# Ordering the scaling of the residual rows behind the convolution in the up projection

## The chip, the core and the metric

The kernel runs on one core of a Trainium2 chip. The time is what the device takes for one execution, in microseconds (us), as the median of several runs. The engines of the core that matter here: TensorE (PE, matmuls; its weight loads are listed apart as PEld), VectorE (DVE), ScalarE (ACT), GpSimd (POOL) and SyncE (SP), which issues most DMA loads. Each engine works through its own queue of instructions in order and waits on semaphores for the others.

## What is computed

One decoder layer on 512 positions of width 1024: two attention branches, an output projection, a LayerNorm, and a gated MLP with a causal convolution of width 3 between the up projection and the gate. All of it is float32. The part that the change touches:

```python
x = _layer_norm(DEEPNORM_ALPHA * x + (1.0 + gt1) * attn_out, ln1_g, ln1_b)
u2 = x * (1.0 + sc2) + sh2
h = _causal_depthwise_conv(u2 @ w_up, conv_w, conv_b)
h_gate, h_val = jnp.split(h, 2, axis=-1)
ffn_out = (jax.nn.silu(h_gate) * h_val) @ w_down
x = _layer_norm(DEEPNORM_ALPHA * x + (1.0 + gt2) * ffn_out, ln2_g, ln2_b)
```

The second LayerNorm needs x itself, scaled by the first one's gain and shifted by its bias (both times alpha). The up projection needs it only in the form u2, which is made apart.

## The kernel before

**Stages.** The kernel runs the modulation and the input projection, attention, the output projection, the up projection (here some 375 to 660 us of the span), and the last products of the down projection with the second LayerNorm.

**Precision.** Each float32 operand is split into a high part (ACT, a cast, for instance wh, line 217) and a low part (DVE, a subtraction at line 94, for instance wl). A product is three matmuls, high by high, low by high and high by low (lines 152 to 154), so every third matmul of a tile in the up projection reads wl.

**Tiles of the up projection.** The loop over n = 0 to 43 (`for n in range(2 * FT)`) makes 44 tiles of 128 channels by 512 positions, each with 24 matmuls of 128x512 into one PSUM bank taken by `bank()`. There are eight banks. From n = 7 on, six of them are held by the accumulators of `early_products`, which adds 18 matmuls after every fourth tile (n = 7, 11, 15, ...; lines 1148 to 1150). The tiles take the remaining two in turn.

**Convolution.** Each tile is followed by its convolution: one ACT instruction (line 1201) and two DVE instructions (lines 1202 and 1203) that read the bank. The list `convs` holds the second DVE instruction of each tile. After every second tile comes the gate (lines 1209 and 1210); after every fourth, the blocks of the down product (lines 1129 to 1132) and their splits (fo, hv).

**Scaling of the residual rows.** `x1` holds four blocks of 128 positions, in two halves of 512 channels each. `o_x1(i, e)` multiplies one half by the gain row (line 975) and adds the bias row (line 976), both on DVE. With its first call it loads the two rows in halves, broadcast over 128 partitions (`ln_row`: four loads on SyncE, line 913, and four scalings on ACT, lines 916 and 919). The loop calls it at every second tile from n = 6 to 20. What uses the result are the sums of the last phases (`fold`, line 1234).

**Other work of DVE in this stage.** The sums of weight blocks for the down product (`pair_proc`, lines 997 to 1002, with splits wdl), the weighted sums of the modulation (`mod_sum`, line 240), and a row of gates (lines 646 and 649).

**Order.** SyncE's queue follows the program. The other engines' instructions are put in order by a scheduler when the program is built: it takes what it expects to be ready, and what is written first needn't stand first. `tc.issue_after(x)` makes what is recorded inside it stand behind x.

Of the kernel before, what the change touches and what calls it, by code (L numbers as in the profile page):

```python
# [12 lines left out]
ALU = mybir.AluOpType  # L13
# [38 lines left out]
def layer_kernel(ctx: ExitStack, tc: tile.TileContext, out, xT, x, c8, wa0, wa1, bcol, w1, wct, wv, bf,  # L52
# [3 lines left out]
    V, S, G, PE = nc.vector, nc.scalar, nc.gpsimd, nc.tensor  # L56
# [20 lines left out]
    def bank():  # L77
        return pp.tile([P, 512], F32, name=nm("ps"), tag="ps")
# [78 lines left out]
    reads, held, pins, convs = [], [], {}, []  # L157
# [752 lines left out]
    def ln_row(n):  # L910
        t = [z(F32, "lnr") for _ in range(2)]
        for e in range(2):
            nc.sync.dma_start(t[e], lnrow[n : n + 1, e * 512 : (e + 1) * 512].broadcast_to([P, 512]))
        if n % 2 == 0:
            for e in range(2):
                S.activation(t[e], t[e], AF.Copy, scale=-0.5 * ALPHA)
        else:
            for e in range(2):
                S.activation(t[e], t[e], AF.Copy, scale=ALPHA)
        return t  # L920
# [3 lines left out]
    x1 = []  # L924
    lnr = []
# [46 lines left out]
    def o_x1(i, e):  # L972
        if not lnr:
            lnr.extend([ln_row(0), ln_row(1)])
        V.tensor_tensor(x1[i][e], x1[i][e], lnr[0][e], ALU.mult)
        V.tensor_tensor(x1[i][e], x1[i][e], lnr[1][e], ALU.add)

    def raw_proc(r):
        return r
# [191 lines left out]
    for n in range(2 * FT):  # L1171
        if n < NSPLIT:
            h, l = items[wui[n]][4]
            ps = bks[n]
            up_mm(ps, h, l, slice(256, 512))
        else:
            ps = bank()
            h, l = weights(wui[n], min(LOADS - 1, wui[min(n + 2, 2 * FT - 1)] - wui[n]))
            up_mm(ps, h, l, slice(0, 512))
            if n % 2 == 0 and 6 <= n < 22:  # L1180
                o_x1((n - 6) // 4, n // 2 % 2 == 0)
            if n >= 7 and n % 4 == 3:
                early_products((n - 7) // 4)
            if n in (10, 28):
                weights(wai[n], 0)
            if n in (10, 30):
                rows = gate_rows(1 + n // 30, G)
                next(rows)
            if n in (11, 32):
                next(rows)  # L1190
        if n == 24:
            for i in range(2):
                lnr2.append(lnp.tile([P, D], F32, name=f"ln2_{i}", tag=f"ln2_{i}"))
                nc.sync.dma_start(lnr2[i], lnrow[2 + i : 3 + i, :].broadcast_to([P, D]))
        if n == 28:
            S.activation(lnr2[0], lnr2[0], AF.Copy, scale=-0.5)
        if n in (30, 32):
            S.dma_start(out[(n - 30) * 64 : (n - 30) * 64 + P, :], lnr2[1])
        t = z(F32, "cv")
        hc.append(t)  # L1200
        S.activation(t, ps, AF.Identity, bias=cw[:, n, 3:4], scale=cw[:, n, 2:3])  # L1201
        V.scalar_tensor_tensor(t[:, 1:], ps[:, 0:511], cw[:, n, 1:2], t[:, 1:], ALU.mult, ALU.add)  # L1202
        convs.append(V.scalar_tensor_tensor(t[:, 2:], ps[:, 0:510], cw[:, n, 0:1], t[:, 2:], ALU.mult, ALU.add))  # L1203
        if n > 3:
            next(work, None)
        if n % 2 == 1:
            g, v = hc
            hc = []
            S.activation(g, g, AF.Silu)  # L1209
            V.tensor_tensor(g, g, v, ALU.mult)  # L1210
            hs.append(g)
            if n % 4 == 3:
                work = blocks(*hs)
                hs = []
                if n < 2 * FT - 1:
                    next(work)
# [102 lines left out]
    lnr = lnr2  # L1319
# [110 lines left out]
```

## Time and profile before

| | |
|---|---|
| median of 3 runs | 735.07 us (734.85 to 735.47) |
| profiled execution | 734.44 us |
| its span | 732.6 us |
| PE busy | 723.3 us, 99% of the span |
| DVE busy | 600.7 us, 82% |
| ACT busy | 391.6 us, 53% |
| granted clock of PE, mean | 0.998 |

The profile is of one execution, and its times count from the start of its span. An engine's busy time counts each stretch in which at least one instruction runs. Matmuls are pipelined, so that the row of a matmul (0.39 us) overlaps the next; how fast PE is going shows in the starts. On DVE too the next instruction may start some 0.08 us before the row of the last one ends, so that the distance between two starts is a little less than a duration. What matters of a wait is whose wait it is: an idle DVE costs nothing as long as PE goes on.

### The profile page before, as it was taken

Reading aid. Unit: us, or ns where it says so; the run is one execution under the profiler, and the core shown is the slowest. Engines: PE = TensorE matmul, PEld = TensorE weight load, DVE = VectorE, ACT = ScalarE, POOL = GpSimd, SP = SyncE. Lnnn points to the kernel's source line nnn. Section 1 sums busy time; section 2 is a strip of 40 time slices with the busy share of each in tenths; the row PEclk is TensorE's granted clock in tenths of the full one; section 3 lists DMA queues with packets and bytes.
Section 4 is the critical chain, followed back from the end, with each engine's and each line's share of the span. In section 5 each row is a group of like instructions: output and inputs, shape, how many; then the busy total and the mean of one; then the engine's idle time right before and its main releaser. Section 6 shows DMA issues by size and latency. Waiting matters only on the chain.

```text
span 732.6 us, 9845 instructions
## 1 busy us (share of the span) xinstructions
PE 723.3 (99%) x3444; PEld 602.2 (82%) x3444; DVE 600.7 (82%) x1041; ACT 391.6 (53%) x684; POOL 87.9 (12%) x142
## 2 busy tenths in 40 slices
PE   8999999999999999999999999999999999999996
PEld 5878888888888888888889888888888888888885
DVE  7978799778898886873687999977887787679996
ACT  5576466686885754442056553454453444347550
POOL 1045224352010000000000001000011010000010
PEclk9999999999999999999999999999999999999999
DMA  9953535423332241632075677577799777656734
GB/s 357 404 207 126 174 116 198 148 88 115 118 116 103 71 171 59 221 130 86 1 259 146 209 248 245 166 247 229 206 339 254 211 239 208 200 161 226 223 86 95
DMA packets 45490, 131.96 MB, mean 180 GB/s; under 512 B 6168, under 2 KB 7200, under 8 KB 45440
## 3 DMA queue, kind: packets, MB, share of 16 engines
q1 hardware_dynamic: 38176, 112.61, 44.7%
q0 software_dynamic: 4224, 10.30, 7.0%
q10 hardware_dynamic: 3040, 8.42, 3.1%
q8 instruction: 27, 0.44, 0.2%
q14 instruction: 23, 0.19, 0.1%
HBM read 118.39 MB, written 12.85 MB: 179 GB/s over the span
## 4 chain that ended last, share of the span: by engine, by line
PE 97%; DMA 1%; DVE 1%; ACT 0%; issue 0%; DVEq 0%
PE ps L152 19%; PE ps L154 19%; PE ps L153 19%; PE ps L1148 5%; PE ps L1149 5%; PE ps L1150 5%; PE ps L369 5%; PE ps L613 3%; PE ps L595 2%; PE ps L521 2%; PE ps L523 2%; PE ps L522 2%; PE ps L939 2%; PE ps L940 2%; PE ps L941 2%; PE ps L547 1%
## 5 line engine op out<-in xcount | busy, mean ns | idle before, releaser
L217 ACT ACTIVATE wh<-raw 128x1024 fp32r<-128x1024 f32 (+1 forms) x105 | 109.1, 1041 | 106.2 <-PE ps L153 44.3
L94 DVE TENSOR_TENSOR wl<-raw,wh 128x1024 fp32r<-128x1024 f32 (+2 forms) x114 | 137.2, 1204 | 33.2 <-ACT wh L217 32.4
L152 PE MATMUL ps<-u2h,wh 128*128 128x512 f32 (+1 forms) x376 | 141.4, 376 | 0.0
L153 PE MATMUL ps<-u2l,wh 128*128 128x512 f32 (+1 forms) x376 | 141.2, 375 | 0.0
L154 PE MATMUL ps<-u2h,wl 128*128 128x512 f32 (+1 forms) x376 | 141.2, 375 | 0.0
L154 PEld LDWEIGHTS ps<-u2h,wl 128*128 128x128 f32 x376 | 70.8, 188 | 12.8
L152 PEld LDWEIGHTS ps<-u2h,wh 128*128 128x128 f32 x376 | 70.8, 188 | 12.8
L153 PEld LDWEIGHTS ps<-u2l,wh 128*128 128x128 f32 x376 | 70.8, 188 | 12.6
L152 PE MATMUL ps<-uh,wh 128*128 128x512 f32 x200 | 79.5, 398 | 0.0
L154 PE MATMUL ps<-uh,wl 128*128 128x512 f32 x200 | 78.3, 391 | 0.0
L153 PE MATMUL ps<-ul,wh 128*128 128x512 f32 x200 | 77.9, 390 | 0.0
L1201 ACT ACTIVATE cv<-ps,cw 128x512 f32<-128x512 f32 x44 | 34.0, 773 | 46.6 <-PE ps L154 40.2
L1202 DVE SCALAR_TENSOR_TENSOR cv<-ps,cw,cv 128x511 f32<-128x511 f32 x44 | 32.8, 744 | 22.6 <-ACT cv L1201 22.6
L154 PEld LDWEIGHTS ps<-uh,wl 128*128 128x128 f32 x200 | 37.5, 188 | 8.6 <-DVE wl L94 0.3
L153 PEld LDWEIGHTS ps<-ul,wh 128*128 128x128 f32 x200 | 37.6, 188 | 7.4
L152 PEld LDWEIGHTS ps<-uh,wh 128*128 128x128 f32 x200 | 37.5, 188 | 7.4
L240 DVE SCALAR_TENSOR_TENSOR raw<-raw,cbc 128x1024 f32<-128x1024 f32 x32 | 39.5, 1238 | 0.0
L575 POOL TENSOR_TENSOR pt<-pt,om 128x127 f32<-128x127 f32 (+3 forms) x32 | 38.6, 1218 | 1.4 <-DVE om L574 1.3
L181 POOL DMA_DIRECT2D raw<-in_wdp x10 | 8.8, 885 | 245.1 <-DMA raw<-in_wdp 229.2
L1203 DVE SCALAR_TENSOR_TENSOR cv<-ps,cw,cv 128x510 f32<-128x510 f32 x44 | 32.7, 743 | 0.4
L574 DVE TENSOR_TENSOR_SCAN om<-om,dg 128x127 f32<-128x127 f32 (+3 forms) x32 | 28.8, 960 | 3.8 <-ACT om L569 3.8
L1209 ACT ACTIVATE cv<-cv 128x512 f32<-128x512 f32 x22 | 13.9, 631 | 33.0 <-DVE cv L1203 33.0
(245 smaller groups left out, 1550.1 us busy)
## 6 DMA issues: line engine op xcount, KB each, us to landing
raw<-in_wup SPq DMA_DIRECT2D x44, 512.0 KB, 5.1
raw<-in_wa SPq DMA_DIRECT2D x32, 512.0 KB, 3.5
raw<-in_wct SPq DMA_DIRECT2D x25, 512.0 KB, 4.5
raw<-in_wdp SPq DMA_DIRECT2D x20, 512.0 KB, 5.2
wa<-in_wa SPq DMA_DIRECT2D x16, 512.0 KB, 8.7
raw<-in_wdp SPq DMA_DIRECT2D x22, 256.0 KB, 4.6
raw<-t SPq DMA_DIRECT2D x22, 256.0 KB, 4.1
raw<-in_wdp POOLq DMA_DIRECT2D x10, 512.0 KB, 7.3
```

What stands on the lines that cost most here:

```text
L94: state["read"] = V.tensor_tensor(o, i, fl(hi), ALU.subtract)
L152: PE.matmul(ps, wh, ah, start=first, stop=False)
L153: PE.matmul(ps, wh, al, start=False, stop=False)
L154: return PE.matmul(ps, wl, ah, start=False, stop=last)
L217: state["hi"] = S.activation(h[:, 0:cols], r[:, 0:cols], AF.Copy)
L240: state["read"] = V.scalar_tensor_tensor(wt[:, c], wt[:, c], 1.0, cbc[:, c] if by is None else by, ALU.mult, ALU.mult, accum_out=o)
L369: m = PE.matmul(grp[g], w, u, start=j == 0 and n == 0, stop=j == KT - 1 and n == 2)
L575: G.tensor_tensor(pt[b][:, s : e - 1], pt[b][:, s : e - 1], om[:, s + 1 : e], ALU.mult)
L1148: PE.matmul(ps, ah, bh, start=first, stop=False, skip_group_check=onto)
L1149: PE.matmul(ps, ah, bl, start=False, stop=False, skip_group_check=onto)
L1150: return PE.matmul(ps, al, bh, start=False, stop=last, skip_group_check=onto)
L1201: S.activation(t, ps, AF.Identity, bias=cw[:, n, 3:4], scale=cw[:, n, 2:3])
```

## The change

The scaling pairs of `o_x1` are recorded inside `tc.issue_after(convs[-1].ins)`. `convs[-1]` is the second DVE instruction of the convolution of the tile before, since the call stands ahead of the tile's own convolution in the loop. The calls move by two tiles: n = 8 to 22 in place of 6 to 20, every second tile as before, with the same halves in the same order. All instructions are the same ones, 16 scalings, four loads and four ACT scalings. Lines from 976 on count one more.

```diff
--- before.py
+++ after.py
@@ -972,8 +972,9 @@
     def o_x1(i, e):
         if not lnr:
             lnr.extend([ln_row(0), ln_row(1)])
-        V.tensor_tensor(x1[i][e], x1[i][e], lnr[0][e], ALU.mult)
-        V.tensor_tensor(x1[i][e], x1[i][e], lnr[1][e], ALU.add)
+        with tc.issue_after(convs[-1].ins):
+            V.tensor_tensor(x1[i][e], x1[i][e], lnr[0][e], ALU.mult)
+            V.tensor_tensor(x1[i][e], x1[i][e], lnr[1][e], ALU.add)
 
     def raw_proc(r):
         return r
@@ -1177,8 +1178,8 @@
             ps = bank()
             h, l = weights(wui[n], min(LOADS - 1, wui[min(n + 2, 2 * FT - 1)] - wui[n]))
             up_mm(ps, h, l, slice(0, 512))
-            if n % 2 == 0 and 6 <= n < 22:
-                o_x1((n - 6) // 4, n // 2 % 2 == 0)
+            if n % 2 == 0 and 8 <= n < 24:
+                o_x1((n - 8) // 4, n // 2 % 2 == 1)
             if n >= 7 and n % 4 == 3:
                 early_products((n - 7) // 4)
             if n in (10, 28):
```

What the scheduler makes of it, at three places in DVE's queue. A convolution's instruction names its tile by the buffer cv_; xn_ are the residual rows, lnr_ the gain and bias rows. Numbers of buffers differ between the two programs.

First listing: from the convolution of tile 8 (cv_4296 before, cv_4294 now) to that of tile 9 (cv_4350, cv_4348). Before:

```order
L1203 SCALAR_TENSOR_TENSOR cv_4296<-ps_4260,cw,cv_4296 128x510
L94 TENSOR_TENSOR fo_4301<-cv_4187,fh_4300 128x256
L999 TENSOR_TENSOR raw_4309<-raw_4309 128x512
L94 TENSOR_TENSOR wdl_4319<-raw_4309,wdh_4317 128x512
L94 TENSOR_TENSOR wl_4379<-raw_4372,wh_4378 128x1024
L94 TENSOR_TENSOR wdl_4320<-raw_4309,wdh_4318 128x512
L975 TENSOR_TENSOR xn_3452<-xn_3452,lnr_4173 128x512
L646 SCALAR_TENSOR_TENSOR gcol<-modr,bcols 128x4
L1202 SCALAR_TENSOR_TENSOR cv_4350<-ps_4306,cw,cv_4350 128x511
L94 TENSOR_TENSOR hv_4354<-cv_4058,hv_4354 128x256
L1203 SCALAR_TENSOR_TENSOR cv_4350<-ps_4306,cw,cv_4350 128x510
```

Now:

```order
L1204 SCALAR_TENSOR_TENSOR cv_4294<-ps_4246,cw,cv_4294 128x510
L94 TENSOR_TENSOR fo_4299<-cv_4173,fh_4298 128x256
L999 TENSOR_TENSOR raw_4307<-raw_4307,raw_4247 128x512
L94 TENSOR_TENSOR wl_4377<-raw_4370,wh_4376 128x1024
L1000 TENSOR_TENSOR raw_4307<-raw_4307 128x512
L94 TENSOR_TENSOR wdl_4317<-raw_4307,wdh_4315 128x512
L240 SCALAR_TENSOR_TENSOR raw_4374,modr<-raw_4374,cbc 128x1024
L94 TENSOR_TENSOR wdl_4318<-raw_4307,wdh_4316 128x512
L94 TENSOR_TENSOR wl_4381<-raw_4372,wh_4380 128x1024
L1203 SCALAR_TENSOR_TENSOR cv_4348<-ps_4304,cw,cv_4348 128x511
L94 TENSOR_TENSOR hv_4352<-cv_4058,hv_4352 128x256
L1204 SCALAR_TENSOR_TENSOR cv_4348<-ps_4304,cw,cv_4348 128x510
```

Between the two convolutions the scaling L975 and the small L646 are gone, and the first sum (L999, before L998, which stood ahead of tile 8's convolution), the weighted sum L240 and one more wl split have come in.

Second listing: from tile 24's convolution on, with the wl split of tile 26 (wl_5214). Before:

```order
L1203 SCALAR_TENSOR_TENSOR cv_5198<-ps_5160,cw,cv_5198 128x510
L94 TENSOR_TENSOR fo_5203<-cv_5093,fh_5202 128x256
L94 TENSOR_TENSOR wl_5214<-raw_5209,wh_5213 128x1024
L997 TENSOR_TENSOR wg_5217<-raw_5211,gt_4412 128x512
L998 TENSOR_TENSOR raw_5211<-raw_5211,raw_5161 128x512
L999 TENSOR_TENSOR raw_5211<-raw_5211 128x512
```

Now:

```order
L1204 SCALAR_TENSOR_TENSOR cv_5198<-ps_5160,cw,cv_5198 128x510
L94 TENSOR_TENSOR fo_5203<-cv_5093,fh_5202 128x256
L998 TENSOR_TENSOR wg_5217<-raw_5211,gt_4410 128x512
L999 TENSOR_TENSOR raw_5211<-raw_5211,raw_5161 128x512
L94 TENSOR_TENSOR wl_5214<-raw_5209,wh_5213 128x1024
L1000 TENSOR_TENSOR raw_5211<-raw_5211 128x512
```

The product wg and the first sum stand ahead of the wl split now, and stood behind it.

Third listing: the blocks after tile 19, and tile 20's convolution (cv_4973, cv_4971). Before:

```order
L1130 TENSOR_TENSOR sg_926_4931<-cv_4869,cv_4747 128x256
L1131 TENSOR_TENSOR cv_4747<-sg_926_4931,cv_4747 128x256
L1132 TENSOR_TENSOR sg_927_4932<-cv_4747,cv_4869 128x256
L94 TENSOR_TENSOR wl_4989<-raw_4984,wh_4988 128x1024
L94 TENSOR_TENSOR wdl_4944<-raw_4941,wdh_4943 128x512
L94 TENSOR_TENSOR wl_5060<-raw_5053,wh_5059 128x1024
L1202 SCALAR_TENSOR_TENSOR cv_4973<-ps_4937,cw,cv_4973 128x511
L94 TENSOR_TENSOR fo_4978<-cv_4747,fh_4977 128x256
L1203 SCALAR_TENSOR_TENSOR cv_4973<-ps_4937,cw,cv_4973 128x510
```

Now:

```order
L976 TENSOR_TENSOR xn_3668<-xn_3668,lnr_4280 128x512
L1131 TENSOR_TENSOR sg_926_4929<-cv_4867,cv_4745 128x256
L977 TENSOR_TENSOR xn_3668<-xn_3668,lnr_4286 128x512
L1132 TENSOR_TENSOR cv_4745<-sg_926_4929,cv_4745 128x256
L94 TENSOR_TENSOR wl_4987<-raw_4982,wh_4986 128x1024
L1133 TENSOR_TENSOR sg_927_4930<-cv_4745,cv_4867 128x256
L94 TENSOR_TENSOR wl_5058<-raw_5051,wh_5057 128x1024
L94 TENSOR_TENSOR wdl_4942<-raw_4939,wdh_4941 128x512
L1203 SCALAR_TENSOR_TENSOR cv_4971<-ps_4935,cw,cv_4971 128x511
L94 TENSOR_TENSOR fo_4976<-cv_4745,fh_4975 128x256
L1204 SCALAR_TENSOR_TENSOR cv_4971<-ps_4935,cw,cv_4971 128x510
```

A pair of scalings (L976, L977) has come in among the blocks, and the wdl split stands behind the second wl split.

On SyncE's queue the four loads of the gain and bias rows stood ahead of four weight loads (for a weighted sum, for tile 9, and for two blocks of the down weights) and stand behind them now. On GpSimd's queue the four writes and the read of the gate row stand ahead of one accumulating load that they stood behind. On PE some of the early products' matmuls change place with matmuls of the tile next to them. No scaling is left in a crowd ahead of tile 12's convolution, where before the last ten of the sixteen stood among nineteen instructions.

## Rows read from the trace of the kernel before

**Rows 1.** Head of the page: span, then busy time and share of each engine.

```profile
span 732.6 us, 9845 instructions
...
PE 723.3 (99%) x3444; PEld 602.2 (82%) x3444; DVE 600.7 (82%) x1041; ACT 391.6 (53%) x684; POOL 87.9 (12%) x142
```

**Rows 2.** Waits of PE, whole span: waiter <- releaser, total us, times, longest.

```profile
PE ps L229 <- DVE warm L107: 1.2, 1, 1.2
PE ps L229 <- DVE wa L240: 0.3, 1, 0.3
PE ps L369 <- DVE uh L331: 0.3, 1, 0.3
```

**Rows 3.** Table by stretch: length, busy us (instructions) by engine, PEclk, DMA share, GB/s.

```profile
421.60:460.40 38.80, 38.80 (x172) 32.12 (x172) 36.95 (x65) 17.72 (x28) 4.39 (x7) 1.00 0.74 237
...
538.00:576.80 38.80, 38.80 (x173) 32.15 (x172) 33.15 (x56) 20.10 (x34) 5.17 (x7) 1.00 0.93 282
```

**Rows 4.** Instructions on the LayerNorm rows: ns min/median/max, first to last start.

```profile
L975 DVE TENSOR_TENSOR xn<-xn,lnr x8: 677/682/683, 421.6 to 459.0; 128x512 f32<-128x512 f32 x8
...
L913 SPq DMA_DIRECT2D lnr<-in_lnrow x4: 376/400/432, 410.6 to 412.1; - x4
```

**Rows 5.** Timeline of PE at tile 12: start us, us, instruction, [idle before <-releaser].

```profile
453.61 0.39 PE L152 MATMUL ps<-u2h,wh 128*128 128x512 f32 x1
453.84 0.39 PE L153 MATMUL ps<-u2l,wh 128*128 128x512 f32 x1
```

**Rows 6.** Timeline of DVE, end of tile 12's convolution.

```profile
462.45 0.74 DVE L1203 SCALAR_TENSOR_TENSOR cv<-ps,cw,cv 128x510 f32<-128x510 f32 x1
```

**Rows 7.** First sum into the scaled rows: ns min/median/max, first to last start.

```profile
L1234 DVE TENSOR_TENSOR xn<-xn,tm x2: 681/682/682, 675.0 to 678.3; 128x512 f32<-128x512 f32 x2
```

**Rows 8.** Timeline of DVE ahead of and in tile 20's convolution.

```profile
511.80 1.23 DVE L94 TENSOR_TENSOR wl<-raw,wh 128x1024 fp32r<-128x1024 f32 x1 [1.49 <-ACT wh L217]
...
513.93 0.74 DVE L1203 SCALAR_TENSOR_TENSOR cv<-ps,cw,cv 128x510 f32<-128x510 f32 x1
```

**Rows 9.** Timeline of DVE from tile 8's convolution to past tile 9's.

```profile
433.95 0.69 DVE L998 TENSOR_TENSOR raw<-raw,raw 128x512 f32<-128x512 f32 x1 [0.68 <-DMA raw<-in_wdp]
434.56 0.74 DVE L1202 SCALAR_TENSOR_TENSOR cv<-ps,cw,cv 128x511 f32<-128x511 f32 x1
...
437.75 1.22 DVE L94 TENSOR_TENSOR wl<-raw,wh 128x1024 fp32r<-128x1024 f32 x1
438.88 0.69 DVE L94 TENSOR_TENSOR wdl<-raw,wdh 128x512 fp32r<-128x512 f32 x1
439.49 0.68 DVE L975 TENSOR_TENSOR xn<-xn,lnr 128x512 f32<-128x512 f32 x1
...
440.16 0.74 DVE L1202 SCALAR_TENSOR_TENSOR cv<-ps,cw,cv 128x511 f32<-128x511 f32 x1
...
441.16 0.74 DVE L1203 SCALAR_TENSOR_TENSOR cv<-ps,cw,cv 128x510 f32<-128x510 f32 x1
...
445.62 1.18 DVE L240 SCALAR_TENSOR_TENSOR raw<-raw,cbc 128x1024 f32<-128x1024 f32 x1
```

**Rows 10.** Timeline of ACT, first step of tile 8's convolution.

```profile
433.41 0.78 ACT L1201 ACTIVATE cv<-ps,cw 128x512 f32<-128x512 f32 x1 [3.87 <-PE ps L154]
```

**Rows 11.** Timeline of DVE around the wl of tile 26.

```profile
539.58 1.22 DVE L94 TENSOR_TENSOR wl<-raw,wh 128x1024 fp32r<-128x1024 f32 x1
540.71 0.68 DVE L997 TENSOR_TENSOR wg<-raw,gt 128x512 f32<-128x512 f32 x1
541.43 0.69 DVE L998 TENSOR_TENSOR raw<-raw,raw 128x512 f32<-128x512 f32 x1
542.15 0.69 DVE L999 TENSOR_TENSOR raw<-raw 128x512 f32<-128x512 f32 x1
```

**Rows 12.** SyncE's issue of L240's load; landing times of loads into raw.

```profile
433.30 0.33 SPq L174 DMA_DIRECT2D raw<-in_wa  x1
...
DMA to landing us min/median/max: 2.6/4.5/9.8
```

## The prediction

> **What bounds the kernel now.** First the head of the page [rows 1]: TensorE (PE) is busy for 723.3 of 732.6 us, VectorE (DVE) for 600.7. The change touches the up projection, and there DVE above all, so the question is whether PE ever waits for DVE in that stage. Second, the waits of PE over the whole span [rows 2]: there are three, 1.8 us in all, and all three are for tiles of the first microseconds (warm, wa, uh). In the up projection PE waits for nobody. Since a busy row could hide short gaps, third a table of four stretches of equal length, 38.8 us each, from 421.6 us on; the first and the last are shown [rows 3]. The first holds all sixteen scaling instructions [rows 4] (L976 has as many as L975); the others hold none. DVE is busy for 36.95 us in the first and 33.15 in the last, yet PE starts 172 matmuls in the first and 173 in the last, at granted clock 1.00 in both. One matmul follows the other by 0.23 us [rows 5]; a tile's 24 matmuls take 5.44 us, so the pitch is 0.2267, and 38.8 / 0.2267 is 171.1: 172 or 173 starts are what an unbroken row gives. The crowd of scaling instructions costs PE one matmul at most, 0.23 us.
>
> **What PE can wait for.** Two things decide. Six of the eight PSUM buffers hold the early products, so two are left for the tiles: tile n can start only when the second step of the convolution (L1203) of tile n-2 has read its bank. And every third matmul of a tile reads wl, which DVE makes. To place the tiles' starts: four tiles of 24 matmuls and one set of 18 early products make 114 matmuls, 25.84 us. Tile 12 starts at 453.61 [rows 5], so tile 20 at 453.61 + 2 x 25.84 = 505.29 and tile 24 at 531.13. Two tiles further, 10.88 us, are tile 14 at 464.49, tile 22 at 516.17 and tile 26 at 542.01. Tile 11 lies 24 + 18 matmuls, 9.52 us, ahead of tile 12: 444.09.
>
> **What is removed.** Before, the last scaling instructions stand in a crowd ahead of tile 12's convolution. That convolution ends at 462.45 + 0.74 = 463.19 [rows 6], 1.30 us before tile 14 needs its bank at 464.49. Without the crowd it ends earlier; but PE doesn't wait there, so this gives 0 us. All sixteen instructions, some 10.9 us at 0.682, are still there: DVE saves nothing.
>
> **What is added.** The new wait of a pair is one of DVE on itself, for a convolution that ends earlier in the same queue. Queued behind a pair are splits, convolutions and the products' blocks. Nobody waits for the scaled rows until the last phases (the first sum into them is at 675.0 [rows 7]), and the last pair moves only from 459.0 to some 525. Eight pairs stand now in eight stretches of 10.88 us or more, 1.2 us in each. The third listing of the change shows such a place: ahead of tile 20's convolution a pair has come in, and a wdl split has moved behind a wl split. In the trace DVE sits idle there for 1.49 us until 511.80, since this wl split waits for ACT [rows 8]; the idle time takes the pair's 1.2 us. What comes later is the convolution, by the one wdl split (0.61, from 438.88 to 439.49 in rows 9): it ended at 513.93 + 0.74 = 514.67 and will end at 515.28, while tile 22 needs it at 516.17. Room 0.9 us, so cost 0. If the idle time weren't there, it would be 1.2 us later, 516.48, and PE would wait 0.3.
>
> The four loads of the LayerNorm rows move behind four weight loads in SyncE's queue, and their four scalings on ACT with them. They were issued from 410.6 to 412.1 [rows 4], 9.5 us ahead of the first use, which moves back too. The loads that they passed start up to 1.9 us earlier (1.5 and 0.4 for the last issue), those that they now precede as much later. On GpSimd's queue the writes of a gate row pass one accumulating load. No wait of PE ends with any of these; cost 0, and 1.9 us at most where such a load is the last thing that a tile waits for.
>
> **The two tight places.** With the pairs moved the scheduler puts other work elsewhere as well, and from there a loss could come. (a) Tile 9's convolution, first listing. Before, it ends at 441.16 + 0.74 = 441.90 [rows 9], 2.19 us ahead of tile 11. Between tile 8's convolution and it three instructions come in: the first sum L998 (0.61, from 433.95 to 434.56), the weighted sum L240 (1.18) and a wl split (1.13, from 437.75 to 438.88). L975 and L646 leave (0.67, from 439.49 to 440.16). Net 2.25 us: it ends at 444.15, 0.06 us too late. But L998 no longer stands ahead of tile 8's convolution, which then waits for ACT alone; ACT is done at 433.41 + 0.78 = 434.19 [rows 10], 0.37 ahead of 434.56. So the bounds are 0.06 us of waiting and 0.31 of room. I take the room, since the row of work ahead of tile 8's convolution has become shorter by more than it, and cost 0. (b) The wl of tile 26, second listing. Before, it ends at 539.58 + 1.22 = 540.80 [rows 11]; the third matmul of tile 26, the first that reads it, starts at 542.01 + 0.45 = 542.46. Now wg and the first sum stand ahead of it, 0.72 each (540.71, 541.43, 542.15): it ends at 542.24. Room 0.22, cost 0; one more split of 0.61 ahead of it would make it 0.4 us of waiting.
>
> The sum: -0.23 to 0 us for the crowd, 0 to 0.06 at (a), 0 to 0.4 at (b), 0 to 0.3 at tile 22; the likeliest is 0 for each. The profiled execution took 734.44 us with a span of 732.6, and the median of the three runs is 735.07, so 0.6 us lie between executions anyway. Forecast: 735.07 + 0, **735.1 us**.
>
> **The rivals.**
> 1. Short waits of PE: (a), (b) and tile 22 all fail. That is 0.06 + 0.4 + 0.3, about 0.8 us, so 735.8. For it speaks that rooms of 0.2 to 0.3 us are smaller than one DVE instruction; against it, that after one wait of PE every later room is larger by as much. Chance 0.12. It still lies within 0.2%.
> 2. A load ends the wait instead. L240 now stands ahead of tile 9's convolution, and its load comes through SyncE's queue; before, it was issued at 433.30 [rows 12]. L240's turn comes after the same seven instructions that ended at 438.88 before, and the first sum's 0.61: at 439.49. From there to the end of the convolution it is 444.15 - 439.49 = 4.66 us. So from a landing 6.1 us after the issue on, PE waits for it. Loads into raw land after 2.6 to 9.8 us, with 4.5 in the middle [rows 12]. At 9.8 the load lands at 443.1, the convolution ends at 447.76 and PE waits 3.7 us: **738.8 us, slower**. For it speaks that the LayerNorm loads lie in that stretch now; against it, the 1.6 us that the middle value leaves. Chance 0.05.
> 3. PE has room that its busy row hides, and the scaling rows in the crowd take it. The weight loads are busy for 32.12 of 38.80 us in the first stretch, which leaves 17%; but it is 32.15 in the last, which has no scaling rows [rows 3]. So these take 0.03 us of it, or 0.23 by the count of matmuls: 734.8. Only gaps that neither count shows could bring more than 0.2%, some 733.5; chance 0.03. The Trainium skill, Perfetto Trace Analysis, section Identifying the Most-Contended Engine, speaks for it: it says that the busy share of matmuls doesn't tell how near TensorE is to its peak, and that the busy share of weight loads does. By that rule 17% could be had in this stage, 6.6 us in each stretch; the trace agrees that the room is there, and not that these instructions are its cause.
> 4. The change doesn't do what it says. The listings show the pairs moved, so this could only mean that DVE is crowded elsewhere instead, with PE as before: 735.1 too.
>
> **How the numbers follow.** The forecast (with rival 4) has 0.80, rival 1 has 0.12, rival 2 has 0.05 and rival 3 has 0.03. About 0.2%, 1.47 us, is what a measurement of this kernel can tell from no change. The forecast lies within it and rival 1 too, but for 0.01 in which it is worse than its sum: same 0.91, slower 0.06, faster 0.03. The range takes the spread of the runs shown (734.85 to 735.47), the 0.23 us of the crowd below and rival 1 above: 734.6 to 735.9.
>
> **What would show it.** In the profile of the changed kernel: no wait of PE in the up projection; 172 to 173 matmuls in each of the four stretches; scaling rows from some 430 to 525 us; DVE less busy than 36.95 us in the first stretch and busier in the next two. (a) or rival 2 is there if PE waits near 444 for the convolution, (b) if it waits near 542 for a wl, and the reading of PE as full is wrong if the time falls by more than 1.47 us.

## The result, and the profile after

The changed kernel takes 736.17 us (median of 22 runs) where the kernel before takes 734.86 (22 runs beside them): ratio 1.0020, 95% interval 1.0015 to 1.0026. That is 1.3 us slower, 0.18%: inside the 0.2% that was called no change, and outside the forecast range of 734.6 to 735.9. The profiled execution took 736.05 us, with a span of 734.2.

First the row of the engines from the head of the page of the changed kernel, which answers to [rows 1]: PE has the same work in a longer span.

```profile
PE 723.1 (98%) x3444; PEld 602.1 (82%) x3444; DVE 601.2 (82%) x1041; ACT 392.1 (53%) x684; POOL 88.0 (12%) x142
```

Then the waits of PE over the whole span (columns as in [rows 2]). The rows of the first microseconds come out otherwise in every profile. One row besides these is new, and it lies in the up projection.

```profile
PE ps L152 <- DVE cv L1204: 0.3, 1, 0.3
```

The table of the four stretches, as in [rows 3]: PE starts 170 matmuls in the first, where it started 172, and 173 in the three others. DVE falls from 36.95 to 32.91 us in the first and rises to 34.99 in the second: the crowd is gone, as forecast, and the loss is in the same stretch.

```profile
421.60:460.40 38.80, 38.55 (x170) 31.60 (x170) 32.91 (x55) 17.40 (x29) 4.36 (x7) 1.00 0.87 264
460.40:499.20 38.80, 38.80 (x173) 32.15 (x172) 34.99 (x60) 20.37 (x35) 1.43 (x2) 1.00 0.66 210
```

The chain that ended last, in order of time, between 425 and 446 us (start, us, what; pieces of under 0.05 us left out). It says in a row where the time comes from: a weight load in SyncE's queue, that of tile 11, takes 11.52 us; ACT and DVE split it; behind the split DVE works off its queue, with the weighted sum L240 in it; the last of the row is the second step of tile 9's convolution (L1204), and PE starts tile 11 at 445.42.

```profile
425.76 11.52 DMA raw<-in_wup
437.30 1.07 ACT wh L217
438.40 1.23 DVE wl L94
439.62 0.60 DVE raw L1000
440.23 0.60 DVE wdl L94
440.83 0.13 DVE raw L240
440.96 0.93 issue
441.89 0.09 DVE raw L240
441.97 0.60 DVE wdl L94
442.58 1.14 DVE wl L94
443.71 0.66 DVE cv L1203
444.37 0.33 DVE hv L94
444.71 0.67 DVE cv L1204
445.42 0.50 PE ps L152
```

And DVE's timeline ahead of it. The wl of tile 10 stands at 434.20, ahead of tile 8's convolution (435.34); DVE is idle for 1.32 us before it, because ACT in turn had waited for its weight load. It is idle once more, for 0.39 us, ahead of the wl of tile 11 at 438.40; the last of these rows is the second step of tile 9's convolution.

```profile
434.20 1.23 DVE L94 TENSOR_TENSOR wl<-raw,wh 128x1024 fp32r<-128x1024 f32 x1 [1.32 <-ACT wh L217]
435.34 0.74 DVE L1203 SCALAR_TENSOR_TENSOR cv<-ps,cw,cv 128x511 f32<-128x511 f32 x1
...
438.40 1.23 DVE L94 TENSOR_TENSOR wl<-raw,wh 128x1024 fp32r<-128x1024 f32 x1 [0.39 <-ACT wh L217]
...
444.62 0.75 DVE L1204 SCALAR_TENSOR_TENSOR cv<-ps,cw,cv 128x510 f32<-128x510 f32 x1
```

In the kernel before the wl of tile 10 stands ahead of tile 8's convolution too, but earlier, and without idle time before it:

```profile
432.06 1.22 DVE L94 TENSOR_TENSOR wl<-raw,wh 128x1024 fp32r<-128x1024 f32 x1
```

**The account of the wait.** From the first step of tile 8's convolution to the second of tile 9's, DVE took 441.16 - 434.56 = 6.60 us before [rows 9]. Now it is 444.62 - 435.34 = 9.28 (444.62 is the start of L1204 in the timeline; the chain counts it from the end of its forerunner). That is 2.68 more: 2.25 as forecast, and 0.39 of idle time ahead of the wl at 438.40. The row itself begins 0.78 us later (434.56 to 435.34). Of this the start of the execution gives 0.69: the first early product of the block ahead of tile 8 starts at 423.69 in the kernel before and at 424.38 now. So 0.09 is left, where the forecast had a gain of 0.37. Together 2.68 + 0.09 = 2.77 us on a room of 2.19: 0.58 late. PE shows it as the 0.64 us from the product at 444.78 to 445.42 and the 0.33 to the next, in place of 0.23 each: 0.51.

```profile
444.78 0.39 PE L1149 MATMUL ps<-wdh,hv 128*128 128x512 f32 x1
445.42 0.50 PE L152 MATMUL ps<-u2h,wh 128*128 128x512 f32 x1 [0.25 <-DVE cv L1204]
445.75 0.39 PE L153 MATMUL ps<-u2l,wh 128*128 128x512 f32 x1
```

**The loads.** Loads issued between 421 and 437 us (issuer, number, KB, median us from issue to landing), the kernel before first, then the changed one: the weight loads take 10.7 us where they took 5.5 (three are issued, those of tiles 10 to 12; the figure is the middle of the last two, the landing of the first can't be told from the trace), and the accumulating load on GpSimd's queue takes 9.7 where it took 7.6.

```profile
raw<-in_wup SPq DMA_DIRECT2D x3, 512.0 KB, 5.5
raw<-in_wdp POOLq DMA_DIRECT2D x1, 512.0 KB, 7.6
```

```profile
raw<-in_wup SPq DMA_DIRECT2D x3, 512.0 KB, 10.7
raw<-in_wdp POOLq DMA_DIRECT2D x1, 512.0 KB, 9.7
```

These are times from the issue, and the changed kernel issues the loads of tiles 11 and 12 earlier, so they overstate how much later the data are there. Tile 11's load is issued at 425.76 in place of 429.35 and lands at 437.28 in place of 435.14, 1.45 us later when the 0.69 of the start are taken off. What ACT waits for tells the same: its casts wh of tiles 10 and 11, before and after, begin 3.93 and 1.44 us later by that count.

```profile
428.48 1.06 ACT L217 ACTIVATE wh<-raw 128x1024 fp32r<-128x1024 f32 x1 [0.58 <-DMA raw<-in_wup]
435.17 1.06 ACT L217 ACTIVATE wh<-raw 128x1024 fp32r<-128x1024 f32 x1 [0.36 <-DMA raw<-in_wup]
```

```profile
433.10 1.06 ACT L217 ACTIVATE wh<-raw 128x1024 fp32r<-128x1024 f32 x1 [1.60 <-DMA raw<-in_wup]
437.30 1.06 ACT L217 ACTIVATE wh<-raw 128x1024 fp32r<-128x1024 f32 x1 [1.81 <-DMA raw<-in_wup]
```

From 429 to 437 us the DMA engines are busy to 1.04 in the changed kernel and were to 0.85 in the one before. The Trainium skill, DMA: Bandwidth & Descriptors, section Queues, rings and completion order, gives a reason: SyncE's loads have one ring on each of 16 shared engines, an engine takes them in the order of the ring, and it turns between the queues. The trace agrees: what lies behind the LayerNorm rows is late, and what is on the other queue too. How much of it is due to these rows is another matter: in `no_loads` below, which doesn't load them, the three weight loads still take 7.4 us and the accumulating load 9.5.

**A second part, at the end.** From the last matmul on, the kernel before needs 732.6 - 725.12 = 7.5 us and the changed one 734.2 - 726.24 = 8.0. DVE does the same in the same time; SyncE's row of its last three stores takes 1.60 us in place of 1.31 (before and after).

```profile
728.84 1.31 SPq L1252 DMA_DIRECT2D out<-xn  x3
```

```profile
729.97 1.60 SPq L1253 DMA_DIRECT2D out<-xn  x3
```

Matmul by matmul, counted from the first of each trace, the changed kernel is 0.69 us behind ahead of tile 8, 1.23 behind past tile 11, 1.12 past 663 us, and 1.6 at the end of the span. So of the 1.6 us between the two spans 0.7 are the start of this execution, 0.5 tile 11 and 0.5 the end, less 0.1 on the way. The start is chance: by the same count the nineteen profiles besides that of the kernel before lie between 0.1 us ahead of it and 1.1 behind at 400 us, though nothing was changed up to there but one small load, split in two of them.

### The profile page after: what moved, and what is told of

Its sections match the earlier page's. It is cut to its first block, busy times and chain, and to the rows that moved or that the text cites. A ratio compares the mean times of both kernels' runs of the same rounds, so it can differ in the third digit from the quotient of the medians.

```text
span 734.2 us, 9838 instructions
## 1 busy us (share of the span) xinstructions
PE 723.1 (98%) x3444; PEld 602.1 (82%) x3444; DVE 601.2 (82%) x1041; ACT 392.1 (53%) x684; POOL 88.0 (12%) x142
## 4 chain that ended last, share of the span: by engine, by line
PE 88%; DMA 6%; DVE 5%; issue 1%; ACT 1%; SPq 0%; DVEq 0%; ACTq 0%
PE ps L152 17%; PE ps L154 17%; PE ps L153 17%; PE ps L1151 5%; PE ps L1150 5%; PE ps L1149 5%; PE ps L613 3%; DMA wa<-in_wa 3%; PE ps L595 2%; PE ps L369 2%; PE ps L521 2%; PE ps L523 2%; PE ps L522 2%; PE ps L939 2%; PE ps L940 2%; PE ps L941 2%
## 5 line engine op out<-in xcount | busy, mean ns | idle before, releaser
L240 DVE SCALAR_TENSOR_TENSOR raw<-raw,cbc 128x1024 f32<-128x1024 f32 x32 | 39.6, 1241 | 0.0
L1204 DVE SCALAR_TENSOR_TENSOR cv<-ps,cw,cv 128x510 f32<-128x510 f32 x44 | 32.8, 745 | 0.4
```

Of the source, the lines that this page charges most:

```text
L240: state["read"] = V.scalar_tensor_tensor(wt[:, c], wt[:, c], 1.0, cbc[:, c] if by is None else by, ALU.mult, ALU.mult, accum_out=o)
```

## The experiments

Times are medians beside runs of the kernel before on the same chip, whose median lay between 734.50 and 734.76 each time. Every ratio is to those runs, with its 95% interval; it is taken over all runs and so is not quite the quotient of two medians.

### Which part of the change: again, pin_only, shift_only, loads_early

`again` is the changed kernel once more.

> The changed kernel once more, for a second look at its two places of loss. Theory A (the convolution of tile 9 comes late, because the LayerNorm loads now stand ahead of the weight loads of tiles 10 and 11 and because the weighted sum stands ahead of it): about 736.2 us, a wait of PE of 0.2 to 1 us at 444 to 446 us for the second step of a convolution. Theory B (the pairs beside later convolutions cost DVE time): 736.2 too, with waits at more than one tile. Theory C (what was seen in the first 32 us, +0.68 us, is chance and the rest is small): 735.3, no wait at 445.

Measured: 736.84 us against 734.66, 1.0023 (1.0014 to 1.0032). By the count of matmuls it loses 1.7 us at tile 11, and the same 8.0 us lie behind the last matmul. Its wait of PE there:

```profile
PE ps L152 <- DVE cv L1204: 1.4, 1, 1.4
```

`pin_only`, against the kernel before:

```
-        V.tensor_tensor(x1[i][e], x1[i][e], lnr[0][e], ALU.mult)
-        V.tensor_tensor(x1[i][e], x1[i][e], lnr[1][e], ALU.add)
+        with tc.issue_after(convs[-1].ins):
+            V.tensor_tensor(x1[i][e], x1[i][e], lnr[0][e], ALU.mult)
+            V.tensor_tensor(x1[i][e], x1[i][e], lnr[1][e], ALU.add)
```

> The kernel before with the new ordering alone: pairs still called at tiles 6 to 20, loads of the LayerNorm rows at tile 6 as before, but each pair behind the convolution of the tile named last. Theory A: 734.9 us, no wait at 445, since the loads stand where they stood. Theory B: 736.2, since the pairs are as spread as in the changed kernel. Theory C: 734.9 to 735.6, whatever the start gives.

Measured: 734.69, 0.9996 (0.9987 to 1.0005), no wait of PE in the up projection. That is so although the weighted sum stands ahead of tile 9's convolution here too (at 441.12) and DVE waited for a load of the sums ahead of tile 8's:

```profile
435.51 0.69 DVE L999 TENSOR_TENSOR raw<-raw,raw 128x512 f32<-128x512 f32 x1 [1.93 <-DMA raw<-in_wdp]
```

`shift_only`, against the kernel before:

```
-            if n % 2 == 0 and 6 <= n < 22:
-                o_x1((n - 6) // 4, n // 2 % 2 == 0)
+            if n % 2 == 0 and 8 <= n < 24:
+                o_x1((n - 8) // 4, n // 2 % 2 == 1)
```

> The kernel before with the new place alone: pairs called at tiles 8 to 22, and the loads of the LayerNorm rows with them, no ordering behind a convolution (they stand in a crowd at tiles 8 to 12 again). Theory A: about 736 us (735.5 to 737), a wait of PE near 445, since two weight splits and the weighted sum still stand ahead of tile 9's convolution and the loads are as late. Theory B: 734.9. Theory C: 734.9 to 735.6.

Measured: 736.61, 1.0026 (1.0016 to 1.0036); PE waits 0.7 and 0.2 us at 445 and 446. The weight load of tile 10 is late (ACT waits 2.80 us for it), but DVE isn't waiting for it: from 430.54 to 435.35 eight scalings stand in a row ahead of the wl of tile 10 and of tile 8's convolution, and DVE has no idle time there. The last two of them:

```profile
434.15 1.29 DVE L975 TENSOR_TENSOR xn<-xn,lnr 128x512 f32<-128x512 f32 x2
```

`loads_early`, against the changed kernel:

```
+            if n == 6:
+                lnr.extend([ln_row(0), ln_row(1)])
             if n % 2 == 0 and 8 <= n < 24:
```

> The changed kernel with the loads of the LayerNorm rows and their scaling on ACT moved back to tile 6; the pairs stay at tiles 8 to 22 behind their convolutions. Theory A: 734.9 us (within 0.2 of the kernel before), no wait at 445. Theory B: 736.2. Theory C: 734.9 to 735.6.

Measured: 734.54, 0.9996 (0.9987 to 1.0005). Its weight loads land after 4.8 us, and tile 9's convolution ends at 441.54 + 0.75 = 442.29 although the weighted sum stands ahead of it here too (DVE's timeline). But the wl of tile 12, which stands ahead of that convolution in the changed kernel, stands behind it (the last row):

```profile
439.40 1.22 DVE L240 SCALAR_TENSOR_TENSOR raw<-raw,cbc 128x1024 f32<-128x1024 f32 x1
...
441.54 0.75 DVE L1206 SCALAR_TENSOR_TENSOR cv<-ps,cw,cv 128x510 f32<-128x510 f32 x1
...
444.14 1.22 DVE L94 TENSOR_TENSOR wl<-raw,wh 128x1024 fp32r<-128x1024 f32 x1
```

What follows: the loss hangs on the place of `ln_row`, the four loads and their scaling, which the change moves along with the first pair; `loads_early` differs from the changed kernel in nothing else (theory A; B falls). The pairs cost nothing in the two orders in which they are pinned; `shift_only` says less, since its crowd may be part of its loss. And the place does two things at once: the loads come at another time, and the scheduler changes DVE's order with them. In `loads_early` and `pin_only` the wl of tile 12 (1.13 us) stands behind tile 9's convolution, and the first sum (0.61) ahead of tile 8's. So these runs show that the weighted sum ahead of tile 9's convolution is not enough by itself, and don't tell late loads from a longer row on DVE.

### Is the weighted sum needed: sum_short, sum_pin

`sum_short`, against the changed kernel (n is the number of the weighted sum, 24 the one ahead of tile 9's convolution):

```
-                mod_sum((4, 2, 3, 5)[n // 8], n % 8, r, slice(0, D), 0)
+                mod_sum((4, 2, 3, 5)[n // 8], n % 8, r, slice(0, 64 if n == 24 else D), 0, cbc[:, 0:64] if n == 24 else None)
```

> The changed kernel, with the one weighted sum that stands ahead of tile 9's convolution cut to 64 of its 1024 columns (15/16 of that sum left out, so this column of the second gate row is not the right one); loads and queues else as in the changed kernel. Some 1.1 us less on DVE there. Theory A, in sums (the loads' lateness of about 0.9 us and the 1.2 us of the sum both needed): the wait of PE near 445 falls from 0.5 to 1.5 us to 0 to 0.4, time 734.6 to 735.2 us. If the late loads alone decide: 736.2.

Measured: 734.98, 1.0005 (0.9996 to 1.0014), a wait of 0.2 us.

`sum_pin`, against the changed kernel:

```
-            with tc.issue_after(state["turn" if n >= 24 else "read"].ins):
+            with tc.issue_after(convs[-1].ins if n == 24 else state["turn" if n >= 24 else "read"].ins):
```

> The changed kernel, with one more ordering by hand: the weighted sum that stood ahead of tile 9's convolution comes behind the convolution named last when it is written (tile 10's); loads, queues and the rest of DVE's order as in the changed kernel. All is computed. If the place of that sum decides: 734.6 to 735.1 us, a wait of PE at 445 of 0 to 0.4. If late loads cost it anyway: 736.0 or more.

Measured: 735.07, 1.0005 (0.9997 to 1.0014). The weight loads are as late as ever (11.5 us), and PE starts tile 11 with a gap of 0.41 us in place of 0.23:

```profile
444.00 0.39 PE L1149 MATMUL ps<-wdh,hv 128*128 128x512 f32 x1
444.41 0.50 PE L152 MATMUL ps<-u2h,wh 128*128 128x512 f32 x1
```

What follows: most of the loss needs the sum's time in that place. Without it the same late loads cost 0.4 us at tile 11 in this profile (0.6 in that of `sum_short`), against 0.5 and 1.7 in the two of the changed kernel.

The kept traces also tell what the lateness is worth. The changed kernel, `again`, `gate_late` and `after_sp` (both below) have one and the same order on DVE from the wl of tile 10 to tile 9's convolution. The table gives the start of that wl less the lead or lag of the execution's start, the idle time ahead of the wl of tile 11, both together, and what PE lost at tile 11 by the count of matmuls, all in us; the last three rows are the runs without the sum.

| profile | wl of tile 10 | idle | together | lost |
|---|---|---|---|---|
| changed kernel | 433.51 | 0.39 | 433.90 | 0.55 |
| `again` | 434.69 | 0.37 | 435.06 | 1.71 |
| `gate_late` | 434.23 | 0.64 | 434.87 | 1.53 |
| `after_sp` | 434.15 | 0.66 | 434.81 | 1.46 |
| `sum_short` | 434.51 | 0.37 | 434.88 | 0.57 |
| `sum_pin` | 434.17 | 0.65 | 434.82 | 0.36 |
| `sum_pin_sp` | 434.33 | 0 | 434.33 | 0 |

In each of the first four the loss is the fourth column less 433.35, to 0.01 us: what DVE waits longer for the weight loads, PE waits longer too, one for one. Without the weighted sum the limit lies 1.0 to 1.1 us later, which is about that sum's own time (1.15). So the loss is the late loads and the full row together. Another way of making the row shorter, such as the wl of tile 12 behind the convolution, was not run by itself.

Of the 0.4 us that the median of `sum_pin` is above the kernel before, the end takes about as much: 7.9 us from the last matmul on, in place of 7.5.

### What makes the loads late: again_small, again_full, gate_late, no_loads, nl_short

`again_full` and `again_small` load the rows early, and once more at tile 8, whole or 1/8 of them (against the changed kernel, core of it; `ln_load` holds the loads of `ln_row`):

```
+            if n == 6:
+                lnr.extend([ln_load(0), ln_load(1)])
+            if n == 8:
+                for r in range(2):
+                    ln_scale(r, lnr[r])
...
+    def ln_scale(n, t):
+        for e in range(2):
+            nc.sync.dma_start(t[e][:, 0:64], lnrow[n : n + 1, e * 512 : e * 512 + 64].broadcast_to([P, 64]))
```

> Full loads of the LayerNorm rows early, at tile 6; at tile 8, at the very place in SyncE's queue where the changed kernel has its four loads, four loads of the first 64 columns again (a fourth of a MB in eight parts: 1/8 of the bytes), then the scaling on ACT; pairs as in the changed kernel. On DVE the same eight instructions stand ahead of tile 9's convolution as in the changed kernel (two wl, two sums, two wdl, the weighted sum), the wl of tile 10 ahead of tile 8's. Theory A1 (the bytes ahead of the weight loads of tiles 10 and 11 make these land late): 734.5 to 735.0 us, no wait of PE near 445. Theory A2 (the queue on DVE alone makes the convolution late): 736.2 to 736.8 with a wait of 0.5 to 1.5 us there.

> The same, but the four loads repeated at tile 8 have their full 256 KB each, as in the changed kernel. Theory A1: 736.2 to 737.5 us, PE waits near 445 by 0.5 to 2 us. Theory A2: no different from the one with small loads.

Measured: 736.28 with small loads and 736.25 with whole ones, both 1.0020 (1.0011 to 1.0029, and 1.0012 to 1.0029). The small ones did not save what they were to save: one of the four issues took 1.8 us on SyncE (the row gives ns min/median/max), so the weight load behind them was issued at 427.87, and its 4.9 us to landing ended as late as ever.

```profile
L918 SPq DMA_DIRECT2D lnr<-in_lnrow x4: 422/427/1803, 424.6 to 426.0; - x4
```

In that profile the loss came through another load: behind tile 8's convolution DVE waited 2.02 us for a load of the sums.

```profile
439.10 0.69 DVE L997 TENSOR_TENSOR raw<-raw,raw 128x512 f32<-128x512 f32 x1 [2.02 <-DMA raw<-in_wdp]
```

With whole loads the same weight load was issued at 425.76 and took 7.2 us, and DVE's order is another (three wl between the two convolutions). So this pair of runs doesn't separate bytes from DVE's queue, and it doesn't tell what the size of the loads is worth.

`gate_late`, against the changed kernel:

```
-            V.scalar_tensor_tensor(d[:, 0 : j1 - j0], modr[:, 4 + i, j0:j1, 0], -1.0, bcols[:, 4 + i, j0:j1], ALU.mult, ALU.subtract)
+            with tc.issue_after(convs[-1].ins):
+                V.scalar_tensor_tensor(d[:, 0 : j1 - j0], modr[:, 4 + i, j0:j1, 0], -1.0, bcols[:, 4 + i, j0:j1], ALU.mult, ALU.subtract)
```

> The changed kernel with the gate row's two small steps on DVE (L646 and the transposition) ordered behind the convolution named last at tile 10, so that its four small writes on GpSimd's queue come some 19 us later, as in the kernel before; nothing else moves on DVE. If these writes make the weight loads late: 734.6 to 735.2 us. If the LayerNorm loads or the weight loads drawn together do: 736.0 to 736.8, the wait at 445 as in the changed kernel.

Measured: 736.22, 1.0022 (1.0013 to 1.0030), a wait of 1.2 us for L1205, the second step. The four writes come at 450.32 in place of 426.92 and change nothing: they are ruled out.

`no_loads`, against the changed kernel:

```
-        for e in range(2):
-            nc.sync.dma_start(t[e], lnrow[n : n + 1, e * 512 : (e + 1) * 512].broadcast_to([P, 512]))
...
-                S.activation(t[e], t[e], AF.Copy, scale=-0.5 * ALPHA)
+                S.activation(t[e], cbc[:, e * 512 : (e + 1) * 512], AF.Copy, scale=-0.5 * ALPHA)
```

> The changed kernel without any load of the LayerNorm rows: their scaling on ACT reads a tile that is there already (so the scaled rows are not the right ones). On DVE the scheduler then puts the two sums and the weighted sum ahead of tile 8's convolution instead of tile 9's. If the LayerNorm loads are what makes the others late: 734.5 to 735.0 us. If the weight loads drawn together are enough, with the work ahead of tile 8's convolution: 736 to 739, a wait of PE of 1 us or more near 440.

Measured: 738.18, 1.0052 (1.0040 to 1.0065). DVE's timeline: the two sums of L997 and L998 and the weighted sum stand ahead of tile 8's convolution now, and the first of them waits 1.34 us for the accumulating load, which takes 9.5 us. PE waits 1.96 us for this convolution, at tile 10.

```profile
435.74 0.69 DVE L997 TENSOR_TENSOR raw<-raw,raw 128x512 f32<-128x512 f32 x1 [1.34 <-DMA raw<-in_wdp]
...
437.70 1.23 DVE L240 SCALAR_TENSOR_TENSOR raw<-raw,cbc 128x1024 f32<-128x1024 f32 x1 [0.33 <-DMA raw<-in_wa]
```

`nl_short` is `no_loads` with the edit of `sum_short`.

> The kernel without LayerNorm loads, with the weighted sum that stands ahead of tile 8's convolution cut to 64 of 1024 columns as well (so neither the scaled rows nor that column of the gate row are the right ones). It takes 1.1 us from ahead of that convolution, of the 2 us that PE waited and some 3.4 us lost in all: if the place of the sum decides, 736.2 to 737.0 us, with a wait of some 0.9 us left for the two sums that wait for their load. If the sum doesn't matter there: 738.2.

Measured: 736.76, 1.0040 (1.0027 to 1.0054). 1.4 us less, by 1.1 us of work taken away. The wait in its profile is 1.6 us, more than the 0.9 expected: there the sum waited 2.97 us for the accumulating load.

What follows: the bytes of the LayerNorm rows are not needed for a loss. Without any of them the scheduler only moves sums that wait for loads further ahead, and a convolution stands behind them again. That the four loads at tile 6 held the loads behind them back in the kernel before, and with these the sums on DVE, is argued from these orders; no run shows it by itself.

### Other places and queues: one_more1, start10, loads_earlier, loads_pool, loads_twice

`one_more1`, against the changed kernel:

```
+            if n == 8:
+                weights(wui[n] + 1, 0)
             if n % 2 == 0 and 8 <= n < 24:
```

> The changed kernel with one weight load, that of tile 10, drawn ahead of the four LayerNorm loads in SyncE's queue, everything else by the scheduler (two wl and the weighted sum still stand ahead of tile 9's convolution, the two sums ahead of tile 8's). If the lateness of that weight load is needed for the loss: 734.5 to 735.1 us, no wait near 445. If DVE's queue alone is enough: 736, a wait of 0.5 us or more.

Measured: 736.18, 1.0021 (1.0012 to 1.0030). The weight load of tile 10 was in time. The next load in the queue, one of the sums', was now the late one: DVE sat idle 2.2 us for it ahead of tile 8's convolution, PE waited 0.9 us for that and 0.9 for a wh. So the loss is not tied to one load.

`start10` (`10 <= n < 26`, the rest to match):

> The changed kernel with everything two tiles later: pairs at tiles 10 to 24, each behind the convolution of the tile named last, the LayerNorm loads at tile 10, ahead of the weight loads of tile 12. If the loss belongs to the place (tile 9, where the weighted sum and two weight splits meet): 734.5 to 735.1 us. If loads that stand ahead of weight loads cost wherever they stand: 736 or more, with a wait of PE about two tiles later, near 455.

Measured: 738.94, 1.0056 (1.0042 to 1.0069). Both guesses missed: the wait is at 439 to 442, not at 455, since with the loads out of the way the sums move ahead of tile 8's convolution, as in `no_loads`, and wait 4.1 us for their load.

`loads_earlier` (`loads_early` with `n == 4`):

> The changed kernel with the LayerNorm loads at tile 4, two tiles ahead of where the kernel before has them. On DVE the two sums and the weighted sum stand ahead of tile 8's convolution, much as without the loads. If an earlier place of these loads is all that matters: 734.5 to 735.0 us. If the order of DVE ahead of tile 8's convolution decides: 736 to 739, a wait of PE of 1 us or more near 440.

Measured: 740.13, 1.0078 (1.0064 to 1.0091). Only 0.5 us of it is the wait expected near 440 to 444; 1.8 and 1.0 us are waits at 415 to 417 for a wh and a wl of an earlier tile, which the scheduler has put behind a convolution's first step on ACT. So this run says that an earlier place is worse, and not why the one at tile 8 is bad.

`loads_pool` (`G.dma_start` in `ln_row`):

> The changed kernel with its four LayerNorm loads at tile 8 issued on GpSimd's queue, the same bytes at the same place of the program, but not ahead of the weight loads in SyncE's queue. If the place in the queue decides: 734.5 to 735.0 us, no wait near 445. If the bytes alone decide, on whatever queue (the 16 DMA engines are shared): 735.5 to 736.5.

Measured: 743.50, 1.0113 (1.0098 to 1.0129), outside both. On GpSimd's queue the rows land after 10.2 us, and ACT, which has their scaling in its row ahead of tile 8's convolution, stands still for it (waits of ACT, 425 to 442 us). DVE in turn waits there for a load of the sums (5.16 us) and then for the scaling (1.90), and PE 6.5 us for that convolution.

```profile
ACT lnr L916 <- DMA lnr<-in_lnrow: 9.3, 1, 9.3
```

`loads_twice` (each load of `ln_row` issued twice):

> The changed kernel with each of its four LayerNorm loads at tile 8 issued twice, so 2 MB in place of 1 MB ahead of the weight loads. Theory A1: another 3 us or so of lateness, 738.5 to 740 us, a wait of 2.5 to 5 us near 445 or 456. Theory A2: 736.2 to 737, since DVE has the same work.

Measured: 747.19, 1.0170 (1.0156 to 1.0184). It is no double dose: the second load into a tile waits in SyncE's queue until the first has landed, and all behind it waits too (waits of SyncE, 420 to 443 us).

```profile
SPq L914 <- DMA lnr<-in_lnrow: 16.3, 4, 6.2
```

### The end: after_sp, sum_pin_sp

After the last matmul it is 7.5 us in the kernel before, `pin_only`, `loads_early`, `one_more1`, `start10` and `loads_earlier`, 7.8 in `again_small`, `again_full`, `no_loads`, `nl_short`, `loads_pool` and `loads_twice`, and 7.9 to 8.0 in the changed kernel (twice), `shift_only`, `sum_short`, `gate_late` and `sum_pin`. The guess was that it goes by the number of SyncE's instructions. Both runs split one small load of the coefficients in two:

```
-    nc.sync.dma_start(cw, cwb)
+    nc.sync.dma_start(cw[:, 0:16, :], cwb[:, 0:16, :])
+    nc.sync.dma_start(cw[:, 16:, :], cwb[:, 16:, :])
```

> The changed kernel with one small early load on SyncE's queue (the convolution's coefficients) split in two, so that SyncE has an instruction or two more. If the place in SyncE's row of instructions sets the loss at the end: 7.5 us from the last matmul to the end, 735.7 us in all, the wait of PE near 445 as before. If not: 8.0 us and 736.2.

> The changed kernel with the weighted sum behind tile 10's convolution and the same load split in two. If both parts of the loss are found with that: 734.6 us, as the kernel before (within 0.2), 7.5 us at the end. If the end doesn't hang on it: 735.1.

Measured: `after_sp` 735.77, 1.0013 (1.0003 to 1.0022), with 7.9 us at the end; `sum_pin_sp` 735.43, 1.0008 (0.9999 to 1.0017), with 8.4. The guess falls: the end moved, but not as it said. `sum_pin_sp` settles something else. In its profile PE has no wait at all behind the first microseconds, with a wl of tile 10 as late (434.36) as in the changed kernel; it is 0.2 us ahead of the kernel before at the last matmul, and its whole excess is the end (its waits of PE, whole span):

```profile
PE ps L229 <- DVE warm L107: 1.2, 1, 1.2
PE ps L369 <- DVE uh L331: 0.3, 1, 0.3
PE ps L369 <- ACT uh L317: 0.2, 1, 0.2
```

None of the kernels beats the one before by more than the intervals hold.

## Why the prediction was wrong, by its own steps

- **What bounds the kernel** held. PE is full, and every gain of the crowd's removal is 0: `pin_only` and `loads_early`, which have it, are at 0.9996. The pairs cost nothing either, as said.
- **The four loads: "cost 0, and 1.9 us at most where such a load is the last thing that a tile waits for"**: this step failed. It priced their issue on SyncE and asked whether PE waits for one of the loads behind. It did not ask what DVE has behind an instruction that waits for one. The rows that were passed over are ACT's waits for its weight loads, 0.58 and 0.36 us in the kernel before ahead of the wh of tiles 10 and 11; in the changed kernel they are 1.60 and 1.81. Nor did the issue times come out as priced, up to 1.9 us later: less the 0.69 of the start, the weight load of tile 10 was issued 0.7 us later and those of tiles 11 and 12 4.3 and 3.2 us earlier, and all three were there later all the same, by some 3.9, 1.45 and 1.5 us.
- **(a) "So the bounds are 0.06 us of waiting and 0.31 of room. I take the room"**: the place and the net 2.25 us were right, the latter to 0.04. The room was not there. It rested on tile 8's convolution waiting for ACT alone once the first sum had left; but the wl of tile 10 stands there too, in both kernels, and now its load was late (0.46 us lost of the room taken), and the wl of tile 11 was late as well (0.39). Instead of -0.31 it was 0.5 us in one profile and 1.7 in the other. With loads in time the room would have been there, by an estimate from the table above: a wl of tile 10 that is done when ACT is, at 434.19, starts 1.14 us ahead of that (from 434.20 to 435.34 in the changed kernel), at 433.05, which is 0.30 below 433.35. With a room of 0.06 us below zero at one bound and a load just moved ahead of both splits, the chance of 0.12 for this rival was far too small.
- **(b) and tile 22** held: no wait of PE there, and 173 matmuls in each later stretch.
- **Rival 1** (735.8, short waits at three places) is nearest; one place of its three failed, by 0.5 us in one profile and 1.7 in the other, where the sum of all three was 0.8. **Rival 2** had the mechanism, a late load ahead of tile 9's convolution, with the wrong load: L240's own landed at 439.82, and its turn came at 440.74.
- **Rival 3** fell. By the rule of the Trainium skill, Perfetto Trace Analysis, section Identifying the Most-Contended Engine, 17% of this stage could be had; none of the 18 runs got any of it, and the weight loads' share in the first stretch fell to 31.60 of 38.80 us while the kernel lost time.
- **The end** (0.5 us) was in no step. SyncE's stores there are in the same order in both kernels, so nothing in the trace of before pointed to it.

What stays open: how much of the loads' lateness in the changed kernel is the 1 MB of the LayerNorm rows and how much the weight loads that are now drawn together ahead of 429 us; and what sets the 0.3 us on SyncE in front of its last stores. That late loads cost 0 to 0.6 us without the sum is shown (`sum_pin_sp`, `sum_pin`, `sum_short`). That the sum costs nothing without late loads is not shown with the rest of the row in place: in `loads_early` and `pin_only` the first sum stands ahead of tile 8's convolution and the wl of tile 12 behind tile 9's.

## What to carry to other kernels

When a change moves a load in a queue, follow the loads behind it to the engines that wait for them, and then ask what those engines have in their own row behind the waiting instruction: here it was a convolution that frees PE's bank, two hops from the load. A load that seems idle work may be what holds later loads, and the work on them, in place; taking it away is not free either. And a room smaller than one instruction of the engine is no room: take it as a coin toss, not as 0.

## What the hardware showed

PE's clock can drop after a wait, and the loss is then more than the wait. After 2.79 us (`start10`) the matmuls from 442.66 to 445.65 us start 0.43 us apart, with the granted clock at 0.57 and 0.58 in the two stretches behind it, mostly the lower of its two levels (1.2 GHz). After 1.96 us (`no_loads`) it stays at 1.00; after two waits of 1.8 and 1.0 us close behind each other (`loads_earlier`) it is 0.57 from 417 to 421 us. First a stretch of `start10`, then one of `no_loads` (columns as in [rows 3]):

```profile
442.00:444.00 2.00, 2.00 (x6) 1.58 (x7) 1.66 (x4) 2.00 (x5) 0.00 (x0) 0.57 0.88 295
```

```profile
442.00:444.00 2.00, 2.00 (x10) 1.64 (x10) 1.65 (x4) 2.00 (x5) 0.00 (x0) 1.00 1.03 418
```

So by the count of matmuls `start10` lost 4.7 us where PE waited 2.8, and `no_loads` 2.2 where it waited 2.0. The changed kernel's own waits, 0.3 and 1.4 us in the two profiles, had no such drop behind them.
